# Order of the first loads, and a second accumulator ring, in the first stage of a streaming encoder step

## The chip, the core and the metric

The kernel runs on one core of one Trainium2 chip. The metric is device microseconds of one execution: 597.59 us, the median of three runs (596.21 to 597.65). TensorE is PE in the profile's rows, VectorE DVE, ScalarE ACT, GpSimd POOL and SyncE SP. Nearly all loads and stores are issued by SP.

## The reference

One layer of a hybrid encoder over 1024 prompt frames and 64 frames of a running stream, stacked here to 1088 frames of width 1024. What the first stage has to compute is this part:

```python
def project(x, g_norm, w_in, b_f):
    h = rmsnorm(x, g_norm) @ w_in
    q, k, v, gf, zf, u, gp, qm, gm = jnp.split(h, IN_SPLITS, axis=-1)
    logf = jax.nn.log_sigmoid(zf + b_f)
...
y = x + concat(silu(gf) * fox_attend(q, k, v, cumsum(logf)),
               silu(gp) * pool_mix(u), silu(gm) * mem_attend(qm, mk, mv)) @ w_out
```

After it come eight heads of forgetting attention, a pooling mixer, four heads of attention over 256 memory tokens, gates, an output projection and a last RMSNorm. Everything is float32; the outputs include k, v, logf and the memory's k and v.

## The kernel before

A float32 product is made of three matmuls: each operand is split into a rounded high part (`whi`, `xh`) and the rest (`wlo`, `xl`), and high x high, high x low and low x high are added in PSUM. A split takes one instruction for the high part (ACT as a rule) and one subtraction for the low part (DVE or POOL). The norm's factor 1/rms is not multiplied into x; it is applied when a result leaves PSUM. It lies in the tile `rcol`, one column for each 128 frames, and is made from the sums of squares of x in its natural layout (`nat` tiles, function `rstd`), in four small DVE steps around one square root on ACT.

The frames are in three chunks: chunk 2 (frames 768 to 1087, 320 of them), chunk 0 (256) and chunk 1 (512), worked in that order. Tiles of 128 frames are numbered 0 to 8, and tile 8 holds the 64 frames of the running stream: its high and low parts stand side by side in `sx`. The first stage computes the values v and the forget logits (`proj_v`, frames in PSUM's rows, weights in two halves of columns g0 and g1, each in two parts of the contraction), then a chain of small steps for the cumulated forget values, the memory's k and v, and the first four of twenty column tiles of the other projections (`proj_chunk`: q0, k0, q1, k1, each over the three chunks).

Names in the rows: `xr` is x as loaded (transposed), `xh2` and `xl2` its split for chunk 2, `wr_2`, `wr_5` the two parts of g0's weights as loaded (each in two loads), `wr_8`, `wr_11` the two parts of g1's; `whi_3`/`wlo_4`, `whi_6`/`wlo_7`, `whi_9`/`wlo_10`, `whi_12`/`wlo_13` their splits; `s_`, `pp_`, `pt_`, `o_` are PSUM accumulators of four rings of two banks each. `wr_125` is the weight tile of q0, `ck` a part of the cached keys.

The order of the work is not the written one. Every operation is recorded by a planner (class `Planner`), which is flushed twice: once for the first stage, once for all the rest. In a flush it picks, engine by engine, the operation that by its cost table can start first, and among equals the one of lower `rank`, then of the longer path to the end (line 219). Rank is -1 for operations that write the rings `ps`, `pt`, `po` on TensorE, and elsewhere for those that touch the ring `pp` or write the weight pool `wp` (lines 108 and 109). Since all instructions are emitted from one place, they bear line 252 in the rows; tiles tell them apart. Ten matmuls on a zero tile (`WARM`, line 29) run before the first data.

Of the kernel before, what the change touches and what calls it, by code (L numbers as in the profile page):

```python
# [25 lines left out]
BIG = 3.0e38  # L26
MARGIN = 0.4
HB = 1
WARM = 10
CH = [(0, 256), (256, 512), (768, 320)]  # L30
LAST = (2, 1, 0)
NQ = NT + NSA
# [10 lines left out]
class Planner:  # L43
# [5 lines left out]
    def __init__(self, nc, tc):  # L49
        self.nc, self.tc = nc, tc  # L50
        self.ops = []
        self.acc = {}
        self.slots = {}
        self.alloc = {}
        self.users = {}
        self.home = {}
        self.free = {e: 0.0 for e in self.ENG}
        self.lock = {"vector": 0.0, "gpsimd": 0.0}
        self.mode = self.table = None
        self.calm = self.boost = False  # L60
        self.dma = [0.0] * 16
        for e in self.ENG:
            setattr(self, e, _Eng(self, e))
# [31 lines left out]
    def add(self, eng, fn, args, kw):  # L95
        op = Op()
        op.eng, op.fn, op.args, op.kw = eng, fn, args, kw
        op.seq, op.succ, op.npred, op.ready, op.level = len(self.ops), [], 0, 0.0, 0.0
        op.mode = op.table = op.start = op.bytes = None
        op.port = False  # L100
        aps = [(i == 0, a) for i, a in enumerate(args)] + [(k in self.OUTS, a) for k, a in kw.items()]
        aps = [(w, a) for w, a in aps if hasattr(a, "tensor")]
        writes = [a for w, a in aps if w]
        reads = [a for w, a in aps if not w]
        self.cost(op, writes, reads)
        homes = {self.home.get(a.tensor.name) for a in writes + reads}
        into = {self.home.get(a.tensor.name) for a in writes}
        urgent = into & {"ps", "pt", "po"} if eng == "tensor" else "pp" in homes or "wp" in into
        op.rank = -1 if self.boost or urgent and not self.calm else 0
        preds = set()  # L110
        for w, a in aps:
            name, p0, p1, f0, f1 = self.box(a)
            hist = self.acc.setdefault(name, [])
            keep = []
            for h in hist:
                hw, q0, q1, g0, g1, o = h
                hit = q0 <= p1 and p0 <= q1 and g0 <= f1 and f0 <= g1
                if hit and (w or hw) and o is not op:
                    preds.add(o)
                if not (w and hit and p0 <= q0 and q1 <= p1 and f0 <= g0 and g1 <= f1) or o is op:  # L120
                    keep.append(h)
            keep.append((w, p0, p1, f0, f1, op))
            self.acc[name] = keep
            self.users.setdefault(name, []).append(op)
        for o in preds:
            self.link(o, op)
        self.ops.append(op)
        return op
# [144 lines left out]
def tile_hymba_step(  # L273
# [6 lines left out]
    nc = Planner(tc.nc, tc)  # L280
    PSUM = bass.MemoryType.PSUM

    def pool(name, bufs, space=None, to=ctx):
        kw = {} if space is None else {"space": space}
        return _Pool(nc, to.enter_context(tc.tile_pool(name=name, bufs=bufs, **kw)))
# [3 lines left out]
    pp, ps, pt, po = (pool(n, 2, PSUM) for n in ("pp", "ps", "pt", "po"))  # L289
    big = pool("big", 1)  # L290
    wp = pool("wp", 2)
# [5 lines left out]
    def nm(s):  # L297
        uid[0] += 1
        return f"{s}_{uid[0]}"
# [7 lines left out]
    def ppt():  # L307
        return pp.tile([P, 512], F32, tag="pp", name=nm("pp"))
# [4 lines left out]
    def otile():  # L313
        return po.tile([P, 512], F32, tag="o", name=nm("o"))

    def mm(out, lhsT, rhs, start, stop):
        nc.tensor.matmul(out, lhsT=lhsT, rhs=rhs, start=start, stop=stop)
# [44 lines left out]
    warm = otile()  # L362
    for _ in range(WARM):
        mm(warm, wm[:, :P], wm, True, True)
# [48 lines left out]
    def load_v(g, a, wpool_, rpool, steps=(4,), hi_eng=None, lo_eng=None):  # L413
        gw = 264 if g == 0 else 256
        raw = rpool.tile([P, WC], F32, tag="wr", name=nm("wr"), bufs=3)[:, : 4 * gw]
        hi = wpool_.tile([P, WC], F32R, tag="whi", name=nm("whi"))[:, : 4 * gw]
        lo = wpool_.tile([P, WC], F32R, tag="wlo", name=nm("wlo"))[:, : 4 * gw]
        src = (wv0, wv1)[g].rearrange("p k c -> p (k c)")
        v = lambda t: t.rearrange("p (a b) -> p a b", a=4)
        k = 0  # L420
        for w in steps:
            c = slice(k * gw, (k + w) * gw)
            k += w
            nc.sync.dma_start(raw[:, c], src[:, 4 * gw * a + c.start : 4 * gw * a + c.stop])
            if hi_eng is None:
                nc.scalar.copy(hi[:, c], raw[:, c])
            else:
                hi_eng.tensor_copy(hi[:, c], raw[:, c])
            (lo_eng or nc.gpsimd).tensor_tensor(lo[:, c], raw[:, c], hi[:, c], op=ALU.subtract)
            yield v(hi), v(lo)  # L430

    def mm3(acc, trip, n):
        for i, (l, r) in enumerate(trip):
            mm(acc, l, r, i == 0, i == n - 1)

    def split_g(raw, g_s, n, hi, lo, ks=range(KT)):
        for k in ks:
            nc.scalar.activation(hi(k), raw[:, k, :n], AF.Copy, scale=g_s[:, k : k + 1])
            nc.vector.scalar_tensor_tensor(
                lo(k), raw[:, k, :n], g_s[:, k : k + 1], hi(k), op0=ALU.mult, op1=ALU.subtract  # L440
            )
# [23 lines left out]
    def vacc():  # L465
        vt_n[0] += 1
        return (ppt, pst, ppt, pst, otile, ptt, pst)[vt_n[0] % 7]()
# [98 lines left out]
    def f_chain3(gps):  # L566
# [15 lines left out]
        nc.sync.dma_start(gpd[0:96, :], gts[:96, 0:128])  # L582
        nc.sync.dma_start(gpd[96:160, :], gts[:64, 128:256])

    def proj_chunk(w, evac, ci):
        wh, wl = w
        t0, n = CH[ci]
        acc = ppt()
        trip = []
        for k in range(KT):  # L590
            xh, xl = xhi[ci][:, k, :], xlo[ci][:, k, :]
            trip += [(wh[:, k, :], xh), (wh[:, k, :], xl), (wl[:, k, :], xh)]
        mm3(acc[:, :n], trip, 24)
        evac(acc, ci, t0, n)
# [8 lines left out]
    def proj(tidx, evac):  # L603
        w = get_w(tidx)
        for ci in range(3):
            proj_chunk(w, evac, ci)
            next(side[0], None)
# [3 lines left out]
    def proj2(t1, e1, t2, e2):  # L611
        we = [(get_w(t), e) for t, e in ((t1, e1), (t2, e2))]
        for ci in LAST:
            for w, e in we:
                proj_chunk(w, e, ci)
# [74 lines left out]
    with st:  # L690
        xp = pool("xp", 2, to=st)
        xTr = xT.rearrange("(k p) t -> p k t", p=P)
        ws = {0: [], 1: []}
        sx = xp.tile([P, KT, P], F32R, tag="sx", name="sx", bufs=1)
        def load_x(ci):
            t0, n = CH[ci]
            raw = xp.tile([P, KT, 512], F32, tag="xr", name=f"xr{ci}", bufs=2)
            steps = (2, 2, 2, 2) if ci == 2 else (4, 4)
            for i, step in enumerate(steps):
                a = sum(steps[:i])  # L700
                nc.sync.dma_start(raw[:, a : a + step, :n], xTr[:, a : a + step, t0 : t0 + n])
                if ci == 2:
                    if a % 4 == 0:
                        gen = load_v(0, a // 4, wp, xp, (2, 2), None, (nc.vector, nc.gpsimd)[a // 4])
                        ws[0].append(next(gen))
                    else:
                        next(gen)
                split_g(
                    raw, gn_s, n, lambda k: xhi[ci][:, k, :], lambda k: xlo[ci][:, k, :],
                    range(a, a + step),  # L710
                )
                if ci == 2:
                    for o, x in ((0, xhi[2]), (NSA, xlo[2])):
                        nc.vector.tensor_copy(sx[:, a : a + step, o : o + NSA], x[:, a : a + step, 256:])

        def load_r(ci):
            t0, n = CH[ci]
            rstd(xp, xn[t0 : t0 + n], n, t0 // P)
# [12 lines left out]
        def load_c():  # L731
            nc.sync.dma_start(ident, ident_d)
            nc.sync.dma_start(bf_s, bf.unsqueeze(0).to_broadcast([P, 8]))

        def load_w1():
            for a in (0, 1):
                ws[1].append(next(load_v(1, a, xp, xp, (4,), (None, nc.vector)[a])))

        load_x(2)
        load_c()  # L740
        load_w1()
        load_x(0)
        load_r(2)
        proj_v(2)
        load_x(1)
        for ci in (0, 1):
            load_r(ci)
# [22 lines left out]
        for t, (wh, wl) in enumerate(wm):  # L770
            acc = vacc()
# [17 lines left out]
        for t in range(2):  # L789
            acc = vacc()  # L790
# [17 lines left out]
            get_w(t)  # L808
        nc.flush(MARGIN)

    ap_ = pool("ap", 2)

    def small(shape, tag):
# [676 lines left out]
```

## Time and profile before

| | us |
|---|---|
| median of three runs | 597.59 |
| profiled execution | 598.18 |
| its span | 596.4 |
| TensorE busy in the span | 567.7 (95%) |

The profiled execution took 598.18 us, of which the core's span is 596.4 us; the rest lies around the span. All times in rows are in us from the span's start. A matmul's duration in the rows includes its way through the pipeline, so the rate is read from the starts of two neighbours. In slices, `PEclk` is the granted TensorE clock as a share of full speed. By stages the idle time of TensorE is 8.5 us in the first 40 us, 1.1 us from 40 to 160, 0.7 us from 160 to 340, 8.9 us from 340 to 500, none from 500 to 580, and 9.6 us at the end.

### The profile page before, as it was taken

What the parts mean: (1) busy time and instruction counts of PE and PEld (TensorE: products, weight loads), DVE (VectorE), ACT (ScalarE), POOL (GpSimd) and SP (SyncE); (2) the same over time, 40 slices, a digit from 0 to 9 for tenths busy, and PEclk for the clock granted to TensorE, in tenths of its full rate; (3) what the DMA queues carried; (4) which work ended last, traced back from release to release, by engine and by line L of the source; (5) the groups of instructions that cost most, each with busy time, mean ns of one, the idle gap of its engine ahead of it and who ended that gap; (6) DMA issues with size and microseconds to landing.
All of it is one profiled execution on the core that took longest, in us unless ns stands there. A gap on an engine that the chain in (4) does not pass through costs nothing.

```text
span 596.4 us, 11206 instructions
## 1 busy us (share of the span) xinstructions
PE 567.7 (95%) x3815; PEld 519.5 (87%) x3815; DVE 334.9 (56%) x822; ACT 291.5 (49%) x675; POOL 225.8 (38%) x374
## 2 busy tenths in 40 slices
PE   7789999999999999999999998999999988999993
PEld 5789999889999999989999988989898767989983
DVE  5774431113677877666498753863356284656334
ACT  5564631122686877787468633862233242323212
POOL 2302374354755542024276560412312294242200
PEclk9999999999999999999999999999999998999998
DMA  8998754568997985586858757824265436585541
GB/s 302 325 312 304 233 162 155 195 233 276 306 341 246 332 263 165 145 320 205 281 162 301 259 160 251 247 88 140 78 169 135 139 106 172 152 259 177 170 142 71
DMA packets 96450, 126.36 MB, mean 212 GB/s; under 512 B 30434, under 2 KB 68618, under 8 KB 94858
## 3 DMA queue, kind: packets, MB, share of 16 engines
q1 hardware_dynamic: 96106, 125.39, 65.4%
q8 instruction: 30, 0.49, 0.3%
q10 hardware_dynamic: 288, 0.27, 0.1%
q14 instruction: 26, 0.21, 0.1%
HBM read 86.41 MB, written 39.21 MB: 211 GB/s over the span
## 4 chain that ended last, share of the span: by engine, by line
PE 77%; DMA 8%; POOL 4%; DVE 4%; issue 3%; ACT 2%; SPq 1%; DVEq 0%; ACTq 0%; POOLq 0%
PE pp L252 38%; PE s L252 15%; PE o L252 13%; PE pt L252 12%; DMA nat<-in_xn_dram 4%; POOL wl L252 2%; DMA rt<-rsd 1%; POOL wlo L252 1%; DMA kd<-hl 1%; DMA xr<-in_xT_dram 1%; DMA ks<-kd 1%; SPq L252 1%; DVE s L252 1%; POOL s L252 1%; DVE xt L252 0%
## 5 line engine op out<-in xcount | busy, mean ns | idle before, releaser
L252 PE MATMUL pp<-xh,whi 128*128 128x320 f32 (+2 forms) x480 | 149.4, 334 | 3.3 <-DVE kr L252 1.6
L252 PE MATMUL pp<-xh,wlo 128*128 128x512 f32 (+2 forms) x480 | 148.1, 332 | 0.0
L252 PE MATMUL pp<-xl,whi 128*128 128x320 f32 (+2 forms) x480 | 147.8, 329 | 0.0
L252 POOL TENSOR_TENSOR wlo<-wr,whi 128x512 fp32r<-128x512 f32 (+2 forms) x44 | 60.3, 1390 | 104.3 <-ACT whi L252 87.8
L252 PEld LDWEIGHTS pp<-xh,whi 128*128 128x128 f32 x480 | 88.3, 188 | 11.2 <-DVE gr L252 2.2
L252 PEld LDWEIGHTS pp<-xh,wlo 128*128 128x128 f32 x480 | 88.2, 188 | 6.0
L252 PEld LDWEIGHTS pp<-xl,whi 128*128 128x128 f32 x480 | 88.5, 189 | 5.0
L252 DVE TENSOR_TENSOR plo<-pt,phi 128x512 fp32r<-128x512 f32 (+1 forms) x96 | 60.6, 642 | 19.6 <-ACT phi L252 15.2
L252 ACT CAST phi<-pt 128x512 fp32r<-128x512 f32 (+1 forms) x96 | 51.8, 550 | 31.7 <-PE pt L252 18.9
L252 PE MATMUL o<-plo,vs 128*128 128x256 f32 x160 | 50.1, 325 | 0.9 <-DVE plo L252 0.9
L252 ACT CAST whi<-wr 128x1024 fp32r<-128x1024 f32 (+1 forms) x25 | 24.6, 983 | 51.7 <-PE pp L252 49.4
L252 PE MATMUL o<-phi,vs 128*128 128x256 f32 x160 | 47.6, 305 | 0.0
L252 PE MATMUL pt<-ident,Q 128*128 128x128 f32 x248 | 47.4, 272 | 0.0
L252 ACT ACTIVATE Q<-Q,m 128x576 f32<-128x576 f32 (+4 forms) x40 | 38.0, 950 | 13.4 <-DVE m L252 13.3
L252 PE MATMUL s<-ks,qb 128*128 128x512 f32 (+3 forms) x128 | 37.9, 374 | 0.5 <-DVE m L252 0.4
L252 POOL TENSOR_TENSOR P<-P,P 128x512 f32<-128x512 f32 (+2 forms) x17 | 18.9, 1114 | 49.0 <-DMA P<-catd 27.8
L252 PEld LDWEIGHTS pt<-ident,Q 128*128 128x128 f32 x248 | 32.2, 140 | 3.1
L252 PEld LDWEIGHTS o<-plo,vs 128*128 128x128 f32 x160 | 30.3, 189 | 2.2 <-DVE plo L252 1.3
L252 PEld LDWEIGHTS o<-phi,vs 128*128 128x128 f32 x160 | 30.3, 189 | 1.4
L252 DVE CUSTOM_DVE_ANT_0 Q<-s,nc 128x512 f32<-128x512 f32 (+2 forms) x40 | 24.0, 601 | 11.4 <-PE s L252 8.1
L252 DVE TENSOR_TENSOR gr<-pp,rb 128x512 f32<-128x512 f32 (+2 forms) x24 | 12.6, 533 | 31.4 <-PE pp L252 31.3
L252 PE MATMUL pt<-ident,P 128*128 128x128 f32 x152 | 28.9, 272 | 0.0
(255 smaller groups left out, 1368.1 us busy)
## 6 DMA issues: line engine op xcount, KB each, us to landing
qd<-hl SPq DMA_DIRECT2D x24, 576.0 KB, 5.2
wr<-in_wt_dram SPq DMA_DIRECT2D x20, 512.0 KB, 3.8
qa<-qd SPq DMA_DIRECT2D x12, 640.0 KB, 5.3
ks<-kd SPq DMA_DIRECT2D x8, 800.0 KB, 5.7
qb<-qd SPq DMA_DIRECT2D x12, 512.0 KB, 4.2
P<-catd SPq DMA_DIRECT2D x17, 256.0 KB, 3.9
nat<-in_xn_dram SPq DMA_DIRECT2D x8, 512.0 KB, 7.6
kd<-hl SPq DMA_DIRECT2D x16, 256.0 KB, 5.1
```

Source lines behind the costliest of these rows:

```text
L252: getattr(getattr(self.nc, op.eng), op.fn)(*op.args, **op.kw)
```

## The change

Four edits, all of which act in the first flush (the last two lines of the diff restore the old rules for the second):

- Every operation recorded while `first` is set gets rank -3 or -2 unless it is TensorE's: that is the loads and splits of chunk 2 with g0's weights (-3) and of g1's weights (-2). The loads of chunk 0 get rank -1. The calls stand in that order now: chunk 2, g1, chunk 0, then the small constants. A load into `wp` is no longer urgent in the first flush.
- The low parts of g0's second half and of g1's first half are made on DVE instead of POOL.
- The projections of the first stage take their accumulators from the rings `ps` and `pp` in turn instead of `pp` alone.
- Nine matmuls on the zero tile instead of ten.

```diff
-WARM = 10
+WARM = 9
@@ Planner.__init__
+        self.first = self.soon = 0
+        self.late = False
@@ Planner.add
-        urgent = into & {"ps", "pt", "po"} if eng == "tensor" else "pp" in homes or "wp" in into
+        urgent = into & {"ps", "pt", "po"} if eng == "tensor" else "pp" in homes or "wp" in into and (eng != "sync" or self.late)
         op.rank = -1 if self.boost or urgent and not self.calm else 0
+        if self.first and eng != "tensor":
+            op.rank = -self.first
+        if self.soon and eng == "sync":
+            op.rank = -self.soon
@@ tile_hymba_step
+    turn = [0, 2]
+
+    def pacc():
+        turn[0] += 1
+        return (ppt, pst, ptt, otile)[turn[0] % turn[1]]()
+
     def proj_chunk(w, evac, ci):
-        acc = ppt()
+        acc = pacc()
@@ load_x
-                        gen = load_v(0, a // 4, wp, xp, (2, 2), None, (nc.vector, nc.gpsimd)[a // 4])
+                        gen = load_v(0, a // 4, wp, xp, (2, 2), None, nc.vector)
@@ load_w1
-                ws[1].append(next(load_v(1, a, xp, xp, (4,), (None, nc.vector)[a])))
-
+                ws[1].append(next(load_v(1, a, xp, xp, (4,), (None, nc.vector)[a], (nc.vector, None)[a])))
+
+        nc.first = 3
         load_x(2)
+        nc.first = 2
+        load_w1()
+        nc.first = 0
+        nc.soon = 1
+        load_x(0)
+        nc.soon = 0
         load_c()
-        load_w1()
-        load_x(0)
         load_r(2)
@@ after the first flush
+    nc.late = True
+    turn[1] = 1
```

What the planner makes of it stands in the built order of both kernels. On SP, at the start of the program, before:

```order
L252 DMA wr_125_267<-in_wt_dram 128x1024
L252 DMA nat_15_150<-in_xn_dram 128x1024
L252 DMA xr2_135<-in_xT_dram 128x2x320
L252 DMA wr_2_136<-in_wv0_dram 128x528
...
L252 DMA nat_16_151<-in_xn_dram 128x1024
L252 DMA nat_17_152<-in_xn_dram 64x1024
L252 DMA wr_8_142<-in_wv1_dram 128x1024
L252 DMA xr0_148<-in_xT_dram 128x4x256
```

and on SP at the same place in the change (between the second and third row shown stand six more loads of `xr2` and g0's weights, between the last two and the row ahead of them `bf_s`, `ident`, `ck` and `gm_s`):

```order
L258 DMA wr_2_136<-in_wv0_dram 128x528
L258 DMA xr2_135<-in_xT_dram 128x2x320
...
L258 DMA wr_8_142<-in_wv1_dram 128x1024
L258 DMA xr0_148<-in_xT_dram 128x4x256 x2
L258 DMA nat_16_151<-in_xn_dram 128x1024
L258 DMA nat_15_150<-in_xn_dram 128x1024
L258 DMA nat_17_152<-in_xn_dram 64x1024
...
L258 DMA wr_11_145<-in_wv1_dram 128x1024
L258 DMA wr_125_267<-in_wt_dram 128x1024
```

The weight tile of q0 and a `nat` tile have left the head of the queue; all three `nat` tiles of chunk 2 now stand behind the eight loads of chunk 2, `wr_8` and `xr0`, and `wr_11` is load 19 instead of 27.

On DVE, where the factor `rcol` of chunk 2 is made, before:

```order
L252 TENSOR_SCALAR ms_18_153<-ss4_14_149 128x3
L252 RECIPROCAL rcol_120<-rt_19_154 128x3
L252 TENSOR_TENSOR rcol_120<-rcol_120,ms_18_153 128x3
L252 TENSOR_TENSOR rcol_120<-rcol_120,rt_19_154 128x3
L252 RECIPROCAL rcol_120<-rcol_120 128x3
L252 SCALAR_TENSOR_TENSOR xl0_127<-xr0_148,gn_s_107,xh0_124 128x256 x5
L252 TENSOR_SCALAR vr_23_158<-s_20_155,rcol_120 128x256
L252 SCALAR_TENSOR_TENSOR zt_118<-s_20_155,rcol_120,bf_s_110 128x8
L252 SCALAR_TENSOR_TENSOR zt_118<-pp_21_156,rcol_120,bf_s_110 128x8
L252 TENSOR_TENSOR vlo_25_160<-s_22_157,vlo_25_160 64x264
L252 CAST whi_12_146<-wr_11_145 128x1024
```

and in the change:

```order
L258 TENSOR_TENSOR wlo_10_144<-wr_8_142,whi_9_143 128x1024
L258 SCALAR_TENSOR_TENSOR xl0_127<-xr0_148,gn_s_107,xh0_124 128x256
L258 ISA nat_16_151,ss4_14_149<-nat_16_151 128x1024
L258 ISA ss4_14_149 128x1
L258 TENSOR_TENSOR vlo_25_160<-s_22_157,vlo_25_160 64x264
L258 SCALAR_TENSOR_TENSOR xl0_127<-xr0_148,gn_s_107,xh0_124 128x256 x6
L258 CAST whi_12_146<-wr_11_145 128x1024
L258 TENSOR_SCALAR ms_18_153<-ss4_14_149 128x3
L258 RECIPROCAL rcol_120<-rt_19_154 128x3
L258 TENSOR_TENSOR rcol_120<-rcol_120,ms_18_153 128x3
L258 TENSOR_TENSOR rcol_120<-rcol_120,rt_19_154 128x3
L258 RECIPROCAL rcol_120<-rcol_120 128x3
```

The cast of `whi_12`, which waits for the load `wr_11`, stood behind `rcol` and stands ahead of it now.

On PE, around the transposes of `rcol` (into `s_34`), before:

```order
L252 MATMUL pp_40_176<-whi_6_140,xl0_127 128x264
L252 MATMUL pp_40_176<-whi_6_140,xh0_124 128x264
L252 MATMUL pp_40_176<-wlo_7_141,xh0_124 128x264
L252 MATMUL pp_44_180<-whi_9_143,xh0_124 128x256
L252 MATMUL s_34_169<-ident_109,rcol_120 128x64
L252 MATMUL s_31_166<-wlo_10_144,sx_134 128x256
L252 MATMUL s_31_166<-whi_9_143,sx_134 128x256
```

and in the change, after 111 matmuls on data:

```order
L258 MATMUL pp_40_176<-wlo_7_141,xh0_124 128x264
L258 MATMUL o_27_162<-whi_12_146,xh2_126 128x256
L258 MATMUL pt_29_164<-whi_12_146,xh2_126 128x256
L258 MATMUL s_34_169<-ident_109,rcol_120 128x128 x2
L258 MATMUL s_34_169<-ident_109,rcol_120 128x64
L258 MATMUL pp_44_180<-whi_9_143,xh0_124 128x256
L258 MATMUL s_31_166<-whi_9_143,sx_134 128x256
L258 MATMUL s_31_166<-wlo_10_144,sx_134 128x256
```

The first matmuls on `whi_12` have moved from behind the transposes to right ahead of them, and `s_31`, which takes the bank of `s_20`, begins behind them instead of ahead. The last 1094 matmuls of the program stand in the same order in both kernels.

## Rows read from the trace of the kernel before

**Rows 1.** Windows of the core by stage: busy of PE, PEld, DVE, ACT, POOL; PEclk, DMA, GB/s
```profile
0.00:40.00 40.00, 31.51 (x202) 27.02 (x202) 27.03 (x62) 23.85 (x46) 10.16 (x11) 1.00 0.92 311
160.00:340.00 180.00, 179.33 (x1300) 168.21 (x1300) 132.66 (x359) 136.74 (x354) 81.81 (x167) 1.00 0.79 257
...
495.00:500.00 5.00, 5.00 (x18) 3.97 (x18) 2.30 (x4) 2.29 (x4) 0.00 (x0) 0.67 0.91 214
```
**Rows 2.** Timeline of PE, 0 to 40: start, us, instruction, idle time before and its releaser
```profile
8.10 0.59 PE L252 MATMUL s<-whi,xh 128*128 128x264 f32 x1 [2.35 <-ACT whi L252]
...
13.19 0.42 PE L252 MATMUL s<-wlo,xh 128*128 128x264 f32 x1
13.41 0.38 PE L252 MATMUL s<-whi,xl 128*128 128x264 f32 x1
...
17.51 0.38 PE L252 MATMUL o<-whi,xh 128*128 128x256 f32 x1 [2.24 <-ACT whi L252]
...
29.01 0.28 PE L252 MATMUL s<-whi,sx 128*128 128x256 f32 x1
29.13 0.28 PE L252 MATMUL s<-wlo,sx 128*128 128x256 f32 x1
...
39.17 0.39 PE L252 MATMUL s<-whi,xh 128*128 128x264 f32 x1 [1.81 <-DVE vlo L252]
```
**Rows 3.** Timeline of SP, 8 to 22: issues of DMAs
```profile
8.99 0.38 SPq L252 DMA_DIRECT2D xr<-in_xT_dram  x1
...
12.15 0.54 SPq L252 DMA_DIRECT2D ck<-in_ckT_dram  x1
...
17.99 0.33 SPq L252 DMA_DIRECT2D tri<-in_tri_d_dram  x1
...
21.99 0.33 SPq L252 DMA_DIRECT2D wr<-in_wv_dram  x1
```
**Rows 4.** Timeline of ACT, 0 to 18
```profile
5.84 1.06 ACT L252 ACTIVATE nat<-nat 128x1024 f32<-128x1024 f32 x1 [3.17 <-DMA nat<-in_xn_dram]
...
6.90 0.55 ACT L252 ACTIVATE xh<-xr,gn_s 128x320 fp32r<-128x320 f32 x1
...
17.99 0.51 ACT L252 ACTIVATE xh<-xr,gn_s 128x256 fp32r<-128x256 f32 x1 [0.54 <-DMA xr<-in_xT_dram]
```
**Rows 5.** Timeline of POOL, 17 to 46
```profile
17.53 2.39 POOL L252 TENSOR_TENSOR wlo<-wr,whi 128x1024 fp32r<-128x1024 f32 x1 [3.00 <-ACT whi L252]
...
43.92 1.29 POOL L252 TENSOR_TENSOR hm<-ck,hm 128x512 fp32r<-128x512 f32 x1 [13.79 <-ACT hm L252]
```
**Rows 6.** Timeline of DVE, 18 to 40
```profile
18.84 1.10 DVE L252 TENSOR_TENSOR rcol<-rcol,ms 128x3 f32<-128x3 f32 x1
...
22.23 0.48 DVE L252 TENSOR_SCALAR vr<-s,rcol 128x256 f32<-128x256 f32 x1
...
22.76 0.22 DVE L252 SCALAR_TENSOR_TENSOR zt<-pp,rcol,bf_s 128x8 f32<-128x8 f32 x1
...
25.50 0.69 DVE L252 CAST whi<-wr 128x1024 fp32r<-128x1024 f32 x1 [1.62 <-DMA wr<-in_wv_dram]
...
36.92 0.17 DVE L252 TENSOR_SCALAR ms<-ss 128x2 f32<-128x2 f32 x1
37.36 0.17 DVE L252 RECIPROCAL rcol<-rt 128x2 f32<-128x2 f32 x1 [0.27 <-ACT rt L252]
...
39.04 0.14 DVE L252 TENSOR_TENSOR rcol<-rcol,ms 128x2 f32<-128x2 f32 x1
```
**Rows 7.** Waits of PE, 90 to 180: us in total, times, longest
```profile
PE pp L252 <- DVE kr L252: 0.9, 2, 0.5
```
**Rows 8.** Timeline of PE, 493 to 497
```profile
493.65 0.50 PE L252 MATMUL pt<-wh,chi 128*128 128x512 f32 x1 [1.20 <-ACT chi L252]
...
496.00 0.63 PE L252 MATMUL pt<-wh,clo 128*128 128x512 f32 x1
496.42 0.63 PE L252 MATMUL pt<-wh,chi 128*128 128x512 f32 x1
```

## The prediction

> **What bounds the kernel now.** I read the windows first. In the first 40 us TensorE is busy 31.5 us; from 160 to 340 it misses 0.7 us of 180 [rows 1]. So a microsecond won at the head stays won only if nothing behind it waits for something that was not moved forward as well; and the head is where there is something to win. PE's timeline shows of what the idle time there consists: TensorE stands still for 2.35 us before the first matmul on data at 8.10, for 2.24 us at 17.51 (for `whi_9`, the high part of g1's first weights) and for 1.81 us at 39.17 (for the eviction of a bank) [rows 2]. Besides, two neighbours of 264 columns start 0.22 us apart at 13.19, and of 256 columns 0.12 us apart at 29.01: until 13.41 the matmuls run at the lower of the two clock levels, 1.2 GHz, although the granted clock reads 1.00 over those 40 us [rows 1, 2].
>
> Then I asked what the first matmul waited for. ACT's first piece of work is the square of a `nat` tile that lands at 5.84, the first high part of x follows at 6.90 [rows 4]. Ahead of that load stood the q0 weight tile and this `nat` tile, 512 KB each (128 x 1024 of 4 bytes), which no early matmul needs.
>
> The SP rows give the landing times. A load issued at 8.99 as the fourteenth lands at 17.99, when ACT starts on it, and at 17.99 SP issues its twenty-second [rows 3, 4]. I read this as: from the ninth on, an issue waits for the landing of the load eight places earlier. So the issue at 12.15, the eighteenth, dates the landing of the tenth, and the one at 21.99, the twenty-seventh, that of the nineteenth [rows 3]. Between the second landing (5.84) and the tenth (12.15) came 4 x 320 + 4 x 264 = 2336 KB: 370 KB per us. Between the tenth and the nineteenth came 3140 KB in 9.84 us: 319 KB per us.
>
> **The head.** The change takes 1024 KB from in front of x: 1024 / 370 = 2.8 us earlier. The last load of chunk 2, the eighth now, lands at about 9.4 instead of 12.15. The square of `nat` (1.06) leaves the front of ACT too, so the first high part of x is ready at about 5.7 and the first matmul starts at 5.8, 2.3 us earlier. One zero matmul less lies beside that wait and costs or gives nothing: TensorE was free at 8.10 - 2.35 = 5.75 and is free earlier now.
>
> How long the slow matmuls last in the change no row shows. Between 8.10 and 13.41 there were 24 of them, each 0.10 too long: 2.4 us. Now the idle time before the data shrinks from 2.35 to about 0.6; I bound the rest by none and by the same 5.3 us of slowness and take half, 12 of them, 1.2 us.
>
> **The place that decides.** In the change 111 matmuls on data stand before the first one on `whi_12`, and right behind it the transposes of `rcol`, then `s_31`, which needs the bank of `s_20`. They take 12 x 0.22 + 99 x 0.12 = 14.5 us and end at about 20.4. `wr_11` is now the nineteenth load; behind the eighth come 512 + 1024 + 1280 + 64 + 256 + 512 = 3650 KB. At 319 KB per us it lands at 9.4 + 11.4 = 20.8 (at 370 it would be 19.3; if it took as long from its issue, which waits for the eleventh landing at about 13.6, as the slowest load above, 9.0 us, it would be 22.6). From there DVE works in order: the cast of `whi_12` 0.69, to 21.5 [rows 6]; then `ms` to the end of the first reciprocal 0.61 (36.92 to 37.53), to 22.1. The next step, a product of two SBUF tiles, took 0.14 at 39.04, when POOL had been idle since 30.1, but 1.10 at 18.84 and ended at 19.94, just when POOL's subtraction of 17.53 ended at 19.92 [rows 5, 6]. Here POOL starts `wlo_13` on the cast at 21.5 and holds to 23.9 by that row's 2.39. So I take the blocked form: 23.9, two more steps 0.45, `rcol` at 24.4; the result and the logits that free `s_20` another 0.75 (22.23 to 22.98) [rows 6]; `s_31` starts at 25.2. TensorE waits there in pieces for about 4 us.
>
> That is 116 matmuls behind the zero ones. Before, the 117th starts at 29.01 [rows 2]. The lead at this place is 29.0 - 25.2 = 3.8 us, with 5.3 at the early landing and 2.0 at the late one. Neither the 2.3 us of the earlier start nor the slow matmuls enter the sum by themselves: a TensorE that arrives earlier only waits longer here.
>
> The Trainium skill, "DMA: Bandwidth & Descriptors", section "Specifications", gives an HBM limit of about 358 GB/s a core. By it the 3650 KB, 3.74 MB, would land 10.4 us behind the eighth and the lead would be about 4.8; the 319 KB per us of the rows, 327 GB/s, is lower and I stay with it.
>
> **Behind it.** The wait of 1.81 at 39.17 was for the bank of `s_31`: the two steps that empty it stood on ACT and DVE behind squares of `nat` tiles that came late. In the change TensorE reaches the accumulator that takes this bank, `s_42`, 99 matmuls after `s_31` begins, at about 37, and the step that frees it comes at 36 to 38 (x of chunk 1 at 26 to 29, its eight splits, two squares of 1.06, the small steps). I credit 1.4 of the 1.81, bounds 0.9 and 1.8.
>
> The two rings: in the q and k projections TensorE waits 0.9 us in two pieces for the eviction of its own ring [rows 7]. With `ps` and `pp` in turn the first has a whole accumulator in between; the second remains in part, since the last accumulator of k1 now ends one matmul before u0 takes its bank. I credit 0.6, bounds 0 and 0.9.
>
> The splits that moved to DVE: two of 528 columns and one of 1024 lie beside loads, since ACT's high parts pace the head; POOL no longer holds DVE there. I count nothing, bounds 0 and 0.5 each way inside the spread above. The reordered middle: TensorE lost 0.7 in 180 us [rows 1], so I count 0 with 0.7 each way. k0's last matmul stood 274 matmuls ahead of the first attention score and stands 240 ahead now, still some 40 us; nothing.
>
> One cost is new. TensorE stands nearly still from 20.4 to 25.2. In the rows, after pauses of which 1.20 before 493.65 is the longest, 512 columns start 0.42 apart at 496.00: the 1.2 GHz level, with a granted clock of 0.67 over 495 to 500 [rows 1, 8]; after the 2.24 at 17.51 the pace stayed at 0.12 [rows 2]. Eight matmuls ran at that level, 8 x 0.20 = 1.6 us. I count half, 0.8, bounds 0 and 1.6. The Trainium skill, "TensorE: Matmul & The Clock Gate", Part 1, says that "the default state is throttled, and activity releases the throttle": by that rule the longer pause here would bring the whole 1.6, a case of its own below.
>
> The sum: 3.8 + 1.4 + 0.6 - 0.8 = 5.0 us. From the profiled execution's 598.2 that is 593.2; the median shown is 0.6 lower, so I predict 592.6.
>
> **Rivals.**
> - The wait at `s_31` hardly occurs, because `wr_11` lands at 19.3 or DVE's product slips in before POOL's subtraction: 5.3 + 1.8 + 0.9 = 8.0, 589.6. Against it: the cast that releases POOL is the instruction just ahead of the chain. Chance 0.13.
> - The wait eats the head: landing at 22.6 (lead 2.0), the clock falls for the whole 1.6, `s_42` waits as before: 2.0 + 0 + 0.3 - 1.6 = 0.7, so 596.9. For it: three `nat` tiles now stand in front of `wr_11`, and SP's issues wait on landings. Chance 0.13.
> - The clock falls for the whole 1.6 and the rest is as forecast: 592.6 + 0.8 = 593.4. For it: the pause is longer than any in the rows; against it: five matmuls lie inside it, and the 2.24 before 17.51 left the clock up. Chance 0.28.
> - Slower: the same chain with `wr_11` later still. Everything behind the cast on DVE waits with it, `rcol`, the bias columns, the splits of chunk 1. Before, `wr_11` landed at 25.50 [rows 6]. Each microsecond beyond 20.8 costs one, so from 20.8 + 5.0 = 25.8 on nothing is won, and at 28.5 it would be 2.7 slower, 600.3. Against it: it is issued about 8 us earlier than before. Chance 0.07.
> - The change does nothing to the end, because the second flush waits for stores of q0 and k0 whose order moved: 597.6. Against it: TensorE's 0.7 us in 180. Chance 0.05.
> - The forecast itself, 592.6: 0.34. With the case of the clock, from which no total can tell it, it holds 0.62 and 591 to 595.5.
>
> From no change a measurement here tells about 0.3%, 1.8 us. Faster by more: 0.62 + 0.13 and some of the second, 0.80. Within: most of the second and the fourth, 0.13. Slower: 0.07. The range for 8 in 10 leaves out the best and the worst tenth: 589.6 to 596.7.
>
> **What would show it.** Right: the first data matmul at 5.5 to 6.2; `whi_9` without a wait of its own; a wait of PE of 2 to 5 us ending with `rcol` or the logits near 24 to 25, with a DVE step on `rcol` stretched to POOL's end; the 1.81 gone; the time at 160 to 340 unchanged. Wrong: a first matmul after 7, `wr_11` behind 23, or a new idle stretch of PE between 40 and 160, where the forget chain on POOL or the memory's weights would be late.

## The result and the profile after

The change makes the kernel slower: 600.03 us (597.46 to 602.14) against 596.74 (595.18 to 598.12) for the kernel before on the same chip, a ratio of 1.005 with a 95% interval of 1.0037 to 1.0063. The prediction was 592.6. The profiled execution of the change took 602.14, with a span of 600.4, against a span of 596.4 before: 4.0 us to be found. This execution is the longest of the change's thirteen; by the medians it is 3.3 us. One run of the experiment warm_fill took 3170.01 us and is left out of its times.

I read the windows of the change first (busy time of each engine and, in brackets, its instructions; then the granted clock of TensorE, the DMA engines' share and GB/s).

```profile
0.00:40.00 40.00, 31.50 (x214) 27.76 (x215) 27.75 (x64) 24.61 (x46) 5.48 (x9) 0.91 0.92 309
...
140.00:160.00 20.00, 14.90 (x82) 13.47 (x81) 6.74 (x15) 4.41 (x9) 9.52 (x18) 0.85 0.77 234
160.00:180.00 20.00, 20.00 (x124) 18.32 (x123) 11.44 (x38) 11.91 (x33) 11.41 (x22) 0.89 0.91 299
160.00:340.00 180.00, 179.47 (x1297) 169.04 (x1296) 133.40 (x372) 137.14 (x362) 83.05 (x173) 0.99 0.76 247
```

Against [rows 1], the first 40 us hold the same 8.5 us of idle time as before. The granted clock reads 0.91 instead of 1.00, but the reading before leaves out the slow matmuls up to 13.41 [rows 2]. From 160 to 340 TensorE misses 0.5 us, as little as before. Before, TensorE was busy for all of these two stretches:

```profile
140.00:160.00 20.00, 20.00 (x125) 18.12 (x124) 11.67 (x38) 8.90 (x24) 12.23 (x20) 1.00 0.88 274
160.00:180.00 20.00, 20.00 (x144) 18.40 (x144) 15.93 (x48) 16.71 (x38) 11.71 (x20) 1.00 1.02 347
```

So the change has a new stall at 140 to 160: 5.1 us of idle time and 0.85 of the clock, and then, with 0.89 of the clock, 20 matmuls fewer at 160 to 180.

One event can be set beside itself in every kernel of this study, the first eviction of qm0 on DVE (start, duration, operation, shapes, and in brackets the idle time ahead of it). It lies just ahead of the stall. Of the kernel before, and of the change:

```profile
140.61 0.42 DVE L252 SCALAR_TENSOR_TENSOR qr<-pp,rb 128x256 f32<-128x256 f32 x1 [3.77 <-PE pp L252]
```

```profile
138.81 0.42 DVE L258 SCALAR_TENSOR_TENSOR qr<-pp,rb 128x256 f32<-128x256 f32 x1 [3.80 <-PE pp L258]
```

Up to there the change is 1.8 us ahead. From there to the end of the span it takes 461.6 us instead of 455.8, 5.8 more: 5.8 - 1.8 = 4.0. The head gained a little; the stretch behind it, with the stall, lost three times as much. (Each of these places is read from one execution.)

**The head.** PE's timeline of the change (the bracket names what ended the wait):

```profile
5.23 0.39 PE L258 MATMUL s<-whi,xh 128*128 128x264 f32 x1 [0.50 <-ACT xh L258]
...
24.14 0.38 PE L258 MATMUL o<-whi,xh 128*128 128x256 f32 x1 [3.82 <-DVE whi L258]
...
27.04 0.96 PE L258 MATMUL s<-ident,rcol 128*128 128x128 f32 x3 [2.39 <-issue]
28.30 0.41 PE L258 MATMUL s<-whi,sx 128*128 128x256 f32 x1
28.52 0.41 PE L258 MATMUL s<-wlo,sx 128*128 128x256 f32 x1
```

The first matmul on data starts at 5.23 instead of 8.10 [rows 2]. But TensorE stands still for 3.82 us before `whi_12` and for 2.39 before `rcol`, and behind these pauses the matmuls start 0.21 us apart until 31.3, the 1.2 GHz level. On DVE and POOL, what it waited for:

```profile
22.89 1.20 DVE L258 CAST whi<-wr 128x1024 fp32r<-128x1024 f32 x1 [3.26 <-DMA wr<-in_wv_dram]
...
24.64 1.88 DVE L258 TENSOR_TENSOR rcol<-rcol,ms 128x3 f32<-128x3 f32 x1
```

```profile
22.27 1.26 POOL L258 TENSOR_TENSOR hm<-ck,hm 128x512 fp32r<-128x512 f32 x1 [21.08 <-ACT hm L258]
24.16 2.34 POOL L258 TENSOR_TENSOR wlo<-wr,whi 128x1024 fp32r<-128x1024 f32 x1 [0.63 <-DVE ms L258]
```

`wr_11` lands at 22.89. DVE's cast of it overlaps POOL's split of `ck` and takes 1.20 instead of 0.69 [rows 6]. The product on 128x3 elements, which took 0.14 with POOL idle [rows 6], ends with POOL's subtraction, at 26.5.

**The stall.** PE, then ACT, then SP (issues; x8 are eight in a row):

```profile
156.47 0.58 PE L258 MATMUL pp<-xh,whi 128*128 128x256 f32 x1 [4.45 <-ACT whi L258]
158.42 0.58 PE L258 MATMUL pp<-xh,wlo 128*128 128x256 f32 x1 [0.65 <-POOL wlo L258]
```

```profile
154.45 1.02 ACT L258 CAST hl<-qr 128x256 fp32r<-128x256 f32 x3 [6.53 <-DMA kd<-hl]
155.37 1.04 ACT L258 CAST whi<-wr 128x1024 fp32r<-128x1024 f32 x1
```

```profile
137.23 1.00 SPq L258 DMA_DIRECT2D nb<-gpd  x2
138.74 0.56 SPq L258 DMA_DIRECT2D qb<-qd  x1
139.34 0.62 SPq L258 DMA_DIRECT2D nc<-gpd  x1
140.00 0.46 SPq L258 DMA_DIRECT2D vraw<-out_dram  x1
141.96 2.42 SPq L258 DMA_DIRECT2D vraw<-in_cv_dram  x1
144.43 2.53 SPq L258 DMA_DIRECT2D vraw<-out_dram  x1
147.06 5.62 SPq L258 DMA_DIRECT2D kd<-hl  x8
```

Read upwards: TensorE waits for a weight's high part; ACT makes it right behind a cast into `hl`, which waits for stores out of `hl`. There is one `hl` buffer (HB = 1), and the eight stores that empty it of k1's halves are issued at 147.06, behind seven loads of the second stage. Before, SP issued them ahead of those loads:

```profile
136.92 6.53 SPq L252 DMA_DIRECT2D kd<-hl  x8
143.50 1.07 SPq L252 DMA_DIRECT2D nb<-gpd  x2
```

and ACT's cast started at 146.19. The diff touches none of these lines. The planner lists the stores ahead of the loads in both kernels, since the first flush has the stores and the second the loads; in the built order of the change they stand the other way round, so a scheduler below the planner has moved them. Why it did so here is not shown; one_ring shows which edit brings it about.

### The profile page after: what moved, and what is told of

It is laid out like the page before. It is cut to its first block, busy times and chain, and to the rows that moved or that the text cites. A ratio compares the mean times of both kernels' runs of the same rounds, so it can differ in the third digit from the quotient of the medians.

```text
span 600.4 us, 11207 instructions
## 1 busy us (share of the span) xinstructions
PE 568.4 (95%) x3814; PEld 521.1 (87%) x3814; DVE 337.5 (56%) x825; ACT 291.6 (49%) x675; POOL 222.0 (37%) x371
## 4 chain that ended last, share of the span: by engine, by line
PE 71%; DMA 6%; DVE 3%; POOL 2%; SPq 2%; issue 1%; ACT 1%; DVEq 0%; POOLq 0%; ACTq 0%
PE pp L258 32%; PE s L258 15%; PE o L258 13%; PE pt L258 11%; SPq L258 2%; DMA kd<-hl 2%; DMA vraw<-out_dram 2%; DMA wr<-in_wt_dram 1%; POOL wlo L258 1%; DMA ks<-kd 1%; POOL wl L258 1%; POOL hl L258 1%; DVE gr L258 1%; DVE xt L258 0%; DVE s L258 0%
## 5 line engine op out<-in xcount | busy, mean ns | idle before, releaser
L258 PE MATMUL pp<-xh,whi 128*128 128x320 f32 (+2 forms) x432 | 136.2, 335 | 8.0 <-ACT whi L258 4.4
L258 PE MATMUL pp<-xh,wlo 128*128 128x512 f32 (+2 forms) x432 | 135.6, 333 | 0.7 <-POOL wlo L258 0.7
L258 PE MATMUL pp<-xl,whi 128*128 128x320 f32 (+2 forms) x432 | 135.9, 332 | 0.0
L258 PEld LDWEIGHTS pp<-xh,whi 128*128 128x128 f32 x432 | 80.7, 191 | 14.9 <-ACT whi L258 4.7
L258 PEld LDWEIGHTS pp<-xh,wlo 128*128 128x128 f32 x432 | 80.8, 191 | 5.9 <-POOL wlo L258 0.9
L258 PEld LDWEIGHTS pp<-xl,whi 128*128 128x128 f32 x432 | 81.0, 191 | 4.5
L258 POOL TENSOR_TENSOR wlo<-wr,whi 128x512 fp32r<-128x512 f32 (+1 forms) x41 | 55.3, 1368 | 68.1 <-ACT whi L258 58.2
L258 PE MATMUL s<-ks,qb 128*128 128x512 f32 (+3 forms) x128 | 39.2, 374 | 0.0
```

The costliest lines, as they stand in the source:

```text
L258: getattr(getattr(self.nc, op.eng), op.fn)(*op.args, **op.kw)
```

## The experiments

Times are medians; the kernel before, on the same chip, had 596.04 beside the first four, 597.13 beside the next four and 596.79 beside the last two. Ratios, with their 95% interval, are to it; between the groups I compare ratios, on a scale of 597, and the expectations of the last six stand on the scale of 596.04.

**stores_first**: only the order on SP is put back, by one edge that holds the first `nb` load behind the last store of k1. On all engines the only rows of the built order that move are the eight stores.

```
+ r = getattr(getattr(self.nc, op.eng), op.fn)(*op.args, **op.kw)
...
+ if self.late and to.startswith("nb_") and self.pin is not None:
+     self.tc.add_manual_dep(
...
+ elif to.startswith("kd1") and not self.late:
+     self.pin = r.ins.name
```

> The changed kernel with one difference: on SP's queue the eight stores of k1's halves (kd<-hl) stand ahead of seven loads (nb, nb, qb, nc, vraw three times) instead of behind them, as in the kernel before; no other instruction moves on any engine. Theory: these stores hold the only hl buffer, so ACT's cast of qm0, and behind it whi and POOL's wlo, waited for them; ahead of the loads they start at about 138 instead of 147.06, the pauses of TensorE of 4.45 and 0.65 near 157 go, and with them the lower granted clock of 140 to 180 (0.85 and 0.89). 5.1 us and 1 to 2 us of clock: 594 us (593 to 595.5), so the head by itself is worth 1 to 3 us against the kernel before. Rival one: the pause comes from something else that the head moved (the weights of u0, POOL): it stays, 599 to 600.5. Rival two: the seven loads, now 6 us later, make the first scores wait instead: 596.5 to 598.5.

Measured: 593.24 us, ratio 0.9957 (0.9938 to 0.9975). SP, ACT and the windows:

```profile
139.28 6.09 SPq L258 DMA_DIRECT2D kd<-hl  x8
```

```profile
148.19 1.02 ACT L258 CAST hl<-qr 128x256 fp32r<-128x256 f32 x3
```

```profile
20.00:40.00 20.00, 15.34 (x102) 14.51 (x101) 13.88 (x29) 10.18 (x20) 4.89 (x3) 0.83 0.94 317
140.00:160.00 20.00, 19.02 (x117) 17.27 (x116) 10.57 (x29) 7.00 (x17) 14.10 (x27) 1.00 0.89 308
160.00:180.00 20.00, 20.00 (x140) 18.54 (x139) 14.52 (x45) 15.59 (x37) 13.68 (x24) 1.00 0.92 298
```

ACT's cast no longer waits for a store, the idle time at 140 to 160 falls from 5.1 to 1.0, and the clock stays up there. By the ratios 0.0093 or 5.5 us come back, 4.2 to 6.9 with both intervals (the medians lie 6.8 apart, but come from two chips). The theory holds; the rivals (a stall from elsewhere, the loads late in their turn) don't.

**stores_late**: the reverse edge in the kernel before, which holds the same eight stores behind the last `vraw` load; nothing else moves.

> The reverse: the kernel before with the same eight stores behind the same seven loads on SP's queue, nothing else moved. Theory: the pause of about 5 us of TensorE appears at 153 to 160 with a granted clock below 0.95 in 140 to 180, and the kernel takes 5 to 7 us more, less what the waits of 340 to 500 give back: 601.5 us (600 to 604). Rival: the order alone does nothing, since in the kernel before k1's projections end at another time: 596 to 597.5.

Measured: 601.39 us, ratio 1.0088 (1.0068 to 1.0109): the kernel before becomes 5.35 us slower. Its ACT and its windows:

```profile
152.64 0.41 ACT L252 CAST hl<-qr 128x256 fp32r<-128x256 f32 x1 [7.59 <-DMA kd<-hl]
```

```profile
140.00:160.00 20.00, 17.85 (x108) 15.91 (x106) 9.54 (x31) 5.97 (x15) 9.36 (x16) 1.00 0.78 251
```

The same wait of the same cast appears. The time is as expected; of the 5.35 us, this trace shows only a part. Its execution is the shortest of the six, 599.4, with a span 1.2 us longer than the one before: the granted clock stayed at 1.00, and TensorE lost 2.15 us here instead of 5, 2.02 of them in a wait at 155.47 for DVE (tile `m`, ahead of a score). Over the whole span the two runs of 599.4 and 599.48 had a granted clock of 0.989 and 0.987, and the four of 601.34 to 603.13 had 0.982 to 0.984. That the clock fell in those four as it did in the change is likely; no trace shows one of them. By the ratios the place of eight issues on one queue is thus worth 0.0093, 5.5 us, in the change and 0.0088, 5.3 us, in the kernel before.

**early_weights**: stores_first, and `wr_11` in the `hl` buffer, which is free until q0.

```
+ if (g, a) == (1, 1):
+     raw = rp.tile([P, 2, NQ], F32, tag="hl", name=nm("wr"), bufs=HB)
...
```

> As stores_first, and the second half of g1's weights (wr_11) has a buffer of its own (that of hl, unused until q0), so that its load is SP's tenth instead of nineteenth. Theory: what made whi_12 late was the place of this load in the queue behind x0 and three nat tiles; it lands at about 14 instead of 22.9, the pause of 3.82 at 24.14 goes, POOL's subtraction of wlo_13 lies before the steps of rcol, which come at about 24 instead of 26.9, and the granted clock of 20 to 40 stays above 0.95: 2 to 4 us less than stores_first, about 591 us. Rival: x of chunk 1 and the nat tiles behind it, whose landing the same bytes set, decide next: the pause moves to 28 to 41, and the time is that of stores_first within 0.7 us.

Measured: 594.69 us, ratio 0.997 (0.9956 to 0.9983); no gain over stores_first, the rival. DVE shows both halves of it:

```profile
14.23 0.69 DVE L258 CAST whi<-wr 128x1024 fp32r<-128x1024 f32 x1
...
22.62 0.17 DVE L258 TENSOR_SCALAR ms<-ss 128x3 f32<-128x3 f32 x1 [2.50 <-ACT nat L258]
```

and PE where the time went:

```profile
37.08 0.39 PE L258 MATMUL o<-whi,xl 128*128 128x264 f32 x1 [1.85 <-DVE xl L258]
```

The load came as early as meant and the pause before `whi_12` is gone, but now the row sums decide (`ms` waits for ACT's square of a `nat` tile), and then the low parts of chunk 1; behind that second pause the granted clock falls too, 0.88 at 40 to 60. Qm0's first eviction stands at 139.55, against 139.15 in stores_first. With this edit, and with the next, the planner sets other operations anew on every engine, so neither is the one step alone.

**low_on_dve**: stores_first, with `wlo_13` subtracted on DVE.

> As stores_first, and the low part of that same weight tile (wlo_13) is made on DVE instead of POOL, so POOL holds nothing while DVE makes rcol; the load stays the nineteenth. Theory: the product that took 1.88 at 24.64 until POOL's end takes 0.16; against it DVE spends 1.22 on the subtraction first: rcol at about 25.9 instead of 26.9, wlo_13 at 24.8 instead of 26.5, so 1 to 1.7 us less of the pauses near 24 to 28: 592.5 to 593.5 where stores_first gives 594. Rival: the late landing at 22.9 alone sets the rest of the head: same as stores_first within 0.5 us.

Measured: 594.43 us, ratio 0.9974 (0.9957 to 0.9991). DVE:

```profile
24.70 0.16 DVE L258 TENSOR_TENSOR rcol<-rcol,ms 128x3 f32<-128x3 f32 x1
...
43.40 1.22 DVE L258 CUSTOM_DVE_ANT_0 nat<-nat 128x1024 f32<-128x1024 f32 x1 [4.89 <-DMA nat<-in_xn_dram]
```

The mechanism is as said, 0.16 for the product instead of 1.88; the total doesn't move, as the rival had it. What was won waits again at 43, where DVE stands still 4.89 us for the next `nat` tile. In stores_first it starts on that tile a microsecond earlier, after a shorter wait:

```profile
42.39 1.23 DVE L258 CUSTOM_DVE_ANT_0 nat<-nat 128x1024 f32<-128x1024 f32 x1 [1.59 <-DMA nat<-in_xn_dram]
```

By qm0's eviction (139.83) nothing is left.

**one_ring**: the change with one ring for the first stage's projections.

```
- turn = [0, 2]
+ turn = [0, 1]
```

> The changed kernel with turn = [0, 1]: the first stage's projections use the pp ring alone, as before; the rest of the change stays. In the built order k1's eight stores then stand ahead of the seven loads again, without any pin (and the first loads and splits differ a little: x's first piece ahead of g0's weights, wr_11 four places later). Theory: the second ring is what moved the stores, so the pause at 152 to 158 is gone; the rings themselves give at most the 0.6 us that the prediction credits: 593.2 + 0.6 = 593.8 us (593 to 595.5). Rival one: the stall comes from the reordered head: 599 to 600.5. Rival two: two rings are worth more than 1.5 us by themselves: 595 to 597.

Measured: 597.43 us, ratio 1.0006 (0.9984 to 1.0027). Without a pin the built order has the stores ahead again, and the stall is gone:

```profile
140.00:160.00 20.00, 20.00 (x127) 18.34 (x126) 10.46 (x34) 7.46 (x19) 10.99 (x17) 1.00 0.98 275
```

So the second ring is what moved the stores. But the total, 596.4 on the scale of the expectation, agrees with my second rival and not with the theory: without the stall and without the second ring, nothing measurable is left of the gain. Qm0's eviction comes at 141.96, later than before; PE waits 2.61 us at 40.02 for `vlo`, the wait of [rows 2] at 39.17 back again. The planner also sets the head's loads anew, so this is not the rings alone, and not the whole of the change's head either.

**rings_first**: the kernel before with two rings, and the stores held ahead.

> The kernel before with two rings for the first stage's projections and k1's stores held ahead of the seven loads; the loads and splits of the head are not rewritten (the planner sets some of them anew). Theory: the rings by themselves take away most of the 0.9 us that TensorE waited for its own ring: 596.0 - 0.6 = 595.4 us (594.5 to 596.5), so that the gain of stores_first, 2.8, is mostly the head's. Rival: the rings are what gains in stores_first: 593 to 594.3.

Measured: 594.64 us, ratio 0.9958 (0.994 to 0.9976), a gain of 2.5 us with the ratio of stores_first; 593.5 on the scale of the expectation, the rival's figure. With one_ring it says which kernels have the 2.8 us of stores_first: the two that have two rings. It does not say what brings them. Here too the planner moved loads in the head (the first matmul on data starts at 6.90 instead of 8.10), and the trace speaks against the waits for a bank. TensorE's waits from 90 to 180, and qm0's first eviction:

```profile
PE pp L252 <- DVE u L252: 0.9, 1, 0.9
PE pp L252 <- DVE kr L252: 0.7, 1, 0.7
```

```profile
140.17 0.42 DVE L252 SCALAR_TENSOR_TENSOR qr<-pp,rb 128x256 f32<-128x256 f32 x1 [4.06 <-PE pp L252]
```

The 0.9 of [rows 7] has become 0.7, and a wait of 0.9 for `u` is new. Of the 3.2 us by which this span, 593.2, is shorter than that of the kernel before, only 0.4 lie ahead of qm0's eviction and 2.8 behind it, where the rings are no longer two. Part of it may be the granted clock: from 490 to 500 it is 1.00 here and 0.83 before, and over the span it is 0.993 in the median of these runs and 0.988 in the median of the kernel before beside them. That would be 0.005 x 593 = 3.0 us at most, an estimate from these figures that no run here tests.

**warm_fill**: stores_first, and twenty products of zeros for each of the two pauses, given no time in the planner, so that the rest of the order stays. The second twenty stand in their pause; the first twenty came into the queue some 35 matmuls ahead of theirs and push these into it.

```
+ if g and ci == 2 and k == 4 and t == 6:
+     for _ in range(20):
+         nc.tensor.matmul(o, lhsT=wm[:, :m], rhs=wm[:, :gw], start=False, stop=False).dur = 0.0
```

> As stores_first, and TensorE multiplies zeros in the two pauses near 21 and 24 us: 20 matmuls of 256 columns ahead of the first one on whi_12 and 20 behind it, added into the open accumulators. Theory: the 23 matmuls at 0.21 us a piece from 26.7 to 32.2 are there because TensorE stood still before them; kept at work it goes on at 0.12, the granted clock of 20 to 40 rises from 0.83 to over 0.95, and 23 x 0.095 = 2.2 us are won, of which 1 to 2 reach the end: 591.5 us. Rival: the head is set by what the loads bring, so that TensorE, faster there, waits between 35 and 75: the same as stores_first within 0.6 us.

Measured: 592.2 us, ratio 0.9917 (0.9889 to 0.9946), the lowest ratio of a version that computes the layer, 0.0040 or 2.4 us below stores_first. The two intervals overlap a little; taken together they leave 0.4 to 4.4 us. The same zeros in low_on_dve, which makes warm_low below, give 0.0042. PE, and the window:

```profile
22.76 0.39 PE L258 MATMUL o<-whi,xh 128*128 128x256 f32 x1 [0.23 <-DVE whi L258]
...
23.10 2.36 PE L258 MATMUL pt<-wm 128*128 128x256 bf16 x20
25.66 0.60 PE L258 MATMUL s<-ident,rcol 128*128 128x128 f32 x3 [0.20 <-issue]
...
26.66 0.28 PE L258 MATMUL s<-whi,sx 128*128 128x256 f32 x1
26.79 0.28 PE L258 MATMUL s<-wlo,sx 128*128 128x256 f32 x1
```

```profile
20.00:40.00 20.00, 19.39 (x160) 18.37 (x160) 14.13 (x31) 10.46 (x21) 4.93 (x3) 1.00 0.93 316
```

Before `whi_12` 0.23 of idle time is left of 2.25 in stores_first. The two waits end when they did, to 0.2 us; but the matmuls behind them start 0.12 us apart, the clock of 20 to 40 is 1.00 instead of 0.83, and qm0's eviction is at 136.45, 2.7 us ahead of stores_first. (The two spans lie 5.2 us apart: the profiled execution of stores_first is the second longest of its nine, that of warm_fill the shortest; the ratios are the measure.) The theory holds; whether more reaches the end than the 1 to 2 us that I gave it, the interval doesn't tell.

**no_nat**: stores_first without the nine loads of x by rows; the squares are taken of a tile of ones.

> As stores_first, without the nine loads of x by rows (nat, 4352 KB): the sums of squares are taken of a tile of ones, so the result is not the layer's. Theory: the first 70 us are set by the bytes that must land (the DMA engines are 0.92 busy over 0 to 40 in both kernels); with a fifth of them gone the pauses near 21 and 25, the slow stretch behind them and the waits near 52 go: 4 to 7 us less, 586 to 589 us. Rival: the weights of g1 and the chain of the forget gate set the head, and bytes do not matter: 592 to 594.

Measured: 589.64 us, ratio 0.9874 (0.9847 to 0.9902), 0.0083 or 5 us below stores_first, inside the theory's range.

```profile
0.00:40.00 40.00, 35.71 (x256) 32.53 (x257) 32.74 (x84) 30.62 (x62) 6.55 (x10) 0.96 0.90 302
40.00:100.00 60.00, 59.82 (x447) 57.11 (x446) 17.98 (x44) 20.13 (x33) 26.00 (x51) 1.00 0.46 151
```

PE has no wait between 10 and 60, and qm0's eviction is at 134.10. This takes away the bytes and the waits for row sums at once; the next kernel parts them.

**nat_unread**: no_nat, but with the nine loads kept; nothing reads what they bring.

```
  nc.sync.dma_start(t[:m], src[j * P : j * P + m, :])
+ x = t
+ if col != 9:
+     x, t = flat, dump
```

> As no_nat, but the nine nat tiles are loaded all the same and not read: the squares are of a tile of ones (the result is not the layer's). It tells the bytes from the waits for row sums. If the bytes set the head, it takes as long as stores_first, 593 us where the kernel before has 596, and PE waits for x of chunk 1 or its weights again. If the waits for row sums set it, it takes as long as no_nat, 588.5 us on the same scale. I hold the bytes for the larger part: 591.5 to 593.5.

Measured: 593.32 us, ratio 0.9938 (0.9915 to 0.9962). Of the 0.0083 between stores_first and no_nat, 0.0064 or 3.8 us come back with the bytes alone, and those two intervals do not touch; the 0.0019 or 1.1 us left to the waits for row sums are within the uncertainty. The loads themselves are the larger part, as expected; qm0's eviction, at 138.38, says the same. (The planner sets the order anew in both kernels, and the nine loads take places on SP's queue besides bytes; neither is parted here.) The windows of nat_unread, and the DMA queue that carries the loads from 30 to 60 (packets, MB, share of 16 engines), first of nat_unread and then of no_nat:

```profile
20.00:40.00 20.00, 20.00 (x168) 19.80 (x166) 18.50 (x39) 11.65 (x23) 6.59 (x3) 1.00 0.99 338
40.00:100.00 60.00, 57.12 (x422) 53.82 (x421) 21.20 (x51) 23.02 (x41) 22.95 (x48) 1.00 0.60 202
```

```profile
q1 hardware_dynamic: 5621, 9.86, 94.0%
```

```profile
q1 hardware_dynamic: 4399, 6.72, 68.8%
```

From 20 to 40 TensorE has no gap. But the queue is as full as in stores_first (90.8%), and TensorE loses 2.9 us between 40 and 100, where no_nat loses 0.2. Free a wait and leave the loads, and TensorE waits behind them.

**warm_low**: warm_fill, with `wlo_13` subtracted on DVE as in low_on_dve.

> warm_fill and low_on_dve together. rcol comes 0.7 us earlier than in warm_fill, and the clock stays up. If what follows takes it back, as low_on_dve showed, it is the same as warm_fill within 0.7 us, 591 us where the kernel before has 596; if the low clock was what took it back there, 0.7 to 1.5 us less.

Measured: 592.46 us, ratio 0.9932 (0.9906 to 0.9958), no gain over warm_fill's 0.9917, and 0.0042 below low_on_dve's 0.9974. Qm0's eviction is at 137.84, against 136.45. DVE:

```profile
42.81 1.23 DVE L258 CUSTOM_DVE_ANT_0 nat<-nat 128x1024 f32<-128x1024 f32 x1 [4.37 <-DMA nat<-in_xn_dram]
```

The same `nat` tile as in low_on_dve is waited for again, 4.37 us here (warm_fill starts on it at 41.31): what was won at `rcol` is given back there, with the clock up as well as without it.

## Why the prediction was wrong, point by point

- **The step that failed** is the last sentence on k0 in "Behind it", "nothing", with the 0 for the reordered middle: the order of k1's stores against the second stage's loads wasn't looked at. I had followed the q0 and k0 pieces through PE and not the stores of the last projection through SP, whose order a scheduler sets. That the second flush could wait for stores whose order moved was a rival, with 0.05 and a price of 5 us, set up against the wrong tiles (q0 and k0). Its price was 5.5 in the change and 5.3 in the kernel before: stores_first and stores_late show it from both sides. With the stores in their old place the same change gains 2.8 us, half of what I summed up. The sign of being wrong that I named, a new idle stretch between 40 and 160, came true, from another cause. And the rival "Slower" has 600.3 only by luck: it wanted `wr_11` at 28.5, which landed at 22.89.
- **The head starts earlier**: foreseen at 5.8, seen at 5.23. Of the 12 slow matmuls that I bounded there the trace has none: from 5.46 on most starts are 0.12 apart. The 111 matmuls end at 20.3, as forecast.
- **The landing of `wr_11`**: 20.8, with 22.6 as the late bound; it was 22.89 in the change (22.05 in stores_first). Read as in the prediction, SP's sixteenth issue, at 10.04, dates the eighth landing, foreseen at 9.4. The 3650 KB behind it came at 3650 / (22.89 - 10.04) = 284 KB per us, against the 319 that I took.
- **The chain behind it**: the cast 0.69, in fact 1.20, since POOL's split of `ck` was running beside it, which I had left out; the product held up by POOL until its end, as predicted, and low_on_dve confirms that POOL's subtraction holds it. `s_31`, which I had at 25.2, starts at 28.30. The lead against 29.01 [rows 2] is 0.7, not 3.8 and below my bound of 2.0. Of the 3.1 us between, 2.1 are the landing and 0.5 the cast. This is the rival "the wait eats the head" in kind: the landing at its late bound and the full fall of the clock came, the wait at `s_42` did not.
- **That 3.8 us of lead stay won behind it** failed too: early_weights and low_on_dve moved the head's steps forward and gained nothing by qm0's first eviction. What comes next, row sums from `nat` tiles and the splits of chunk 1, is bound to later loads.
- **The 1.81 us at 39.17** are gone in the change, as said. It comes back in one_ring (2.61), so the gain hangs on what two rings bring.
- **The two rings, 0.6**: the wait that they were to shorten fell from 0.9 to 0.7, in the change as in rings_first, so the term is 0.2. Rings_first as a whole is 2.5 faster than the kernel before; most of that lies behind the first stage, and its cause is open.
- **The clock, 0.8 of at most 1.6**: the pace of 0.21 instead of 0.12 lasted for 14 matmuls in the change, 14 x 0.095 = 1.3 us, and for 24, 2.3 us, in stores_first; filled, 2.4 us come back. The full fall was the right choice. Of the Trainium skill, "TensorE: Matmul & The Clock Gate", Part 1, the sentence that I quoted there agrees with these runs: after pauses of 3.82 and 2.39 the level was down, and with zeros in them it was not.

In sum: predicted 5.0 at the head and nothing behind it; seen 1.8 at qm0's first eviction, and 5.8 lost behind it. The 2.8 that are there without the stall are found in the kernels with two rings and not in the one with the rewritten loads alone. So the loads, which I had at 3.8, bring nothing measurable by themselves there; what the second ring brings beyond its 0.2 stays open.

## What to carry to other kernels

Where a scheduler sets the order of a queue, compare the whole built queue of every engine, stores too, and not only the region that the diff speaks of: a ring of one buffer turns the place of its stores into a lock on whoever writes it next. A head that waits for loads was not shortened here by moving one load or one step forward, since the next wait hung on a later load; the loads as a whole set the pace: leaving nine out gave 5 us, freeing the waits for them alone some 1 us, which can't be told from nothing. And a pause that can't be taken away can still be filled: here zeros on TensorE delayed nothing behind the pauses and kept its clock.

## What the runs showed of the hardware

- The same product of two 128x3 tiles on DVE took 0.16 us beside an idle POOL and 1.88 beside POOL's subtraction, until its end (24.64 + 1.88 = 26.52; 24.16 + 2.34 = 26.50). The cast of 1024 columns on DVE took 0.69 in early_weights, with POOL idle, and 1.20 in the change, where POOL's split of `ck` ran until 23.53; in stores_first, with 0.27 us of overlap instead of 0.64, it took 0.82. The Trainium skill, "SBUF — State Buffer", section "SBUF: two separate sides", has it that the two engines share a pair of ports, and that the first to start takes it for its whole instruction, on VectorE's side where the instruction has two inputs from SBUF or works in a two-port mode; the rows agree.
- Behind two pauses of 2 to 4 us close together the clock fell, for 14 matmuls in the change and 24 in stores_first, and twenty zero matmuls in each pause prevented it. The length of a pause alone doesn't settle it: 2.02 in stores_late and 2.24 at 17.51 in the kernel before [rows 2] left it at 1.00, while behind 1.85 at 37.08 in early_weights it fell.
- The times of one kernel spread over some 4 us between runs of the same chip (591.73 to 595.60 for stores_first), so that differences under 1 us between two experiments say nothing; the 1 us or so by which the kernels differ in 340 to 500 is left open.
